# The rows of seven products moved by 180 bytes, and a fourth place in one ring of weights

## The chip, the cores and the metric

The kernel runs on one core of a Trainium2 chip. The metric is the device time of one execution in microseconds; the time given for a kernel is the median of its runs. TensorE (PE) multiplies matrices out of on-chip memory (SBUF) into accumulators (PSUM). VectorE (DVE), ScalarE (ACT) and GpSimd (POOL) work elementwise. SyncE (SP) issues most DMAs; POOL issues the accumulating ones. Each engine takes its own instructions in the order of its queue and waits at semaphores for the others.

## The reference, cut to what matters

One layer of a decoder: 512 tokens, model width 1024, feed-forward width 2816.

```python
def swiglu(x, w_in, w_out):
    a, b = jnp.split(x @ w_in, 2, axis=-1)
    return (jax.nn.silu(a) * b) @ w_out

h = x
h = h + 0.5 * swiglu(rmsnorm(h, ffn1_norm), ffn1_w_in, ffn1_w_out)
h = h + hybrid_mixer(rmsnorm(h, mix_norm), w_in, ...)   # HGRN2 and Gated DeltaNet branches
h = h + 0.5 * swiglu(rmsnorm(h, ffn2_norm), ffn2_w_in, ffn2_w_out)
y = rmsnorm(h, final_norm)
```

All is float32. The change touches the two feed-forward stages above all; the mixer shares their weight places.

## The kernel before, in words

**Three matmuls for one.** A float32 operand is split into a high part, rounded to the format that TensorE takes at full rate (float32r), and a remainder. `mm3` multiplies high by high, high by remainder and remainder by high into one accumulator. In its three lines (195, 196, 197) the stationary operand of the first two is a weight's high part, `whi`, and that of the third its remainder, `wlo`.

**Fast products.** A feed-forward stage computes the first `slow` of its 22 blocks of hidden columns plainly (5 in the first stage, of which two run in an opening of their own, 3 in the second). The others go through `fast`: the two-by-two block product of weights and activations is done as seven products of sums and differences (Strassen's scheme in Winograd's form) instead of eight. The seven activation operands are made once for a stage by `operands` and stand in the tile `xs` (28 rows of 512 columns; four rows for an operand, two of high parts and two of remainders). The matmuls of the fast part write `px` and move 256 columns each.

One product of `fast` is seven *units*, each of 4 x 3 matmuls on one 128 x 512 slab of weights:

| unit | weights | ring | how its remainder is made |
|---|---|---|---|
| 0 | a11 as loaded | 1 | fold |
| 1 | s2 = s1 - a11, s1 = a21 + a22 | 0 | VectorE |
| 2 | a12 as loaded | 1 | fold |
| 3 | s1 | 0 | VectorE |
| 4 | s3 = a11 - a21 | 0 | VectorE |
| 5 | s4 = a12 - s2 | 0 | VectorE |
| 6 | a22 as loaded | 1 | fold where product p < 7 or 15 <= p < 21, else VectorE |

The sums s1 to s4 are VectorE instructions of `comb` (line 371), into four tiles `sw`. For each unit ScalarE casts the slab to `whi` (line 334). Then either VectorE subtracts (`wlo`, line 313), or ScalarE writes the negated high part into `wlo` (line 338) and POOL issues a DMA that adds the weights from memory to it (line 339): the *fold*. The weights of `px` are kept in places of a ring; each ring has three places (WB // 2) for high parts and three for remainders. `pair` hands out the places, 576 columns wide, of which a unit uses 512 from column `off`: 0 for plain units and the mixer, SHIFT = 19 columns (76 bytes) for units of `fast`.

**What sets the order.** `stream` writes out all queues by hand. For each unit t it issues the unit's matmuls, then the functions in `posts[t]` (the product's own follow-up: the copy `p` after unit 0, `fa` after unit 2, its silu after 3, `uu` and `vb` after 4, `uc` after 6, its silu after the next unit 0, and two half-tile gate products, line 473, after the next unit 1; for products from 17 on also the split of the gate into `uh` and `ul`, lines 476 and 477). Then comes `ahead(t, 2)`, which prepares later units: remainders of the units cast in the call before, loads of raw weights (SP), sums for units up to t + COMB - 1 whose weights have been asked for, and then, ring 1 before ring 0, casts of units up to t + LEAD - 1 as far as their ring has a place: unit number m of a ring may be cast once unit m - 3 of the same ring has run.

**After the fast part** the stage multiplies the gated columns by its second weight matrix. The gated columns are split into high part and remainder by `split`, from the sixth-last unit of the fast part on, into rows of `xs` that are no longer read, in the order of the list `freed`.

Of the kernel before, what the change touches and what calls it, by code (L numbers as in the profile page):

```python
# [9 lines left out]
F32R = mybir.dt.float32r  # L10
# [6 lines left out]
P = 128  # L17
T = 512
# [21 lines left out]
WB = 6  # L40
# [14 lines left out]
LAG = dict(raw=3.5, gb=6.5, nb=6, m=7, out=5.5, back=6, turn=5.5)  # L55
EASE = 2.5
TURNED = (0, 1)
SHIFT = 19
LANES = {"a": 2, "b": 2, "d": 1, "e": 1}


# [85 lines left out]
def body(tc, xT, cst, sqc, hmask, dta, w1o, w1a, w2a, wt, wn, wab, wbh, wbg, wo, w1b, w2b, gfin, y, dbg=None):  # L147
# [4 lines left out]
    wp = ctx.enter_context(tc.tile_pool(name="wp", bufs=1))  # L152
# [22 lines left out]

    taken = [0]

    def pair(lane=None, off=0):

        taken[0] += 1  # L180
        n = "wv"[taken[0] % 2 if lane is None else lane]
        return [wp.tile([P, 576], F32R, tag=n + x, name="w" + x, bufs=WB // 2)[:, off:off + 512] for x in ("lo", "hi")]

    def slab(src):
        f = src.shape[-1]
# [73 lines left out]
    class Raw:  # L259

        def __init__(self, src, readers=1, fast=False):
            self.src, self.left, self.fast = src, readers, fast

    class Unit:

        def __init__(self, raws, operand, run, comb=None, drop=(), fold=None, lane=None, off=0):
            self.raws, self.operand, self.run, self.comb, self.drop, self.fold = raws, operand, run, comb, drop, fold
            self.lane, self.off = lane, off

    def plain(src, nk, xs, where, n=T, fold=False, roomy=lambda k: False):  # L270

# [12 lines left out]
            return Unit([raw], lambda: raw.tile[:, :w_ * P], run, drop=(raw,), fold=raw.src if fold and k >= fold - 1 else None)  # L284
        return [unit(k) for k in range(0, nk, 4)], held

    def stream(units, fp, early, hooks, posts):

        waiting = [r for u in units for r in u.raws]
        sent = {False: [], True: []}  # L290
        for i, u in enumerate(units):
            u.lane = i % 2 if u.lane is None else u.lane
        lanes = [[i for i, u in enumerate(units) if u.lane == l] for l in range(2)]
        done, combs, parts, fresh = [0, 0], [0], [None] * len(units), []
        room = [99]

        def loads():
            while waiting and room[0]:
                r = waiting[0]
                n = sent[r.fast]  # L300
                m = RW if r.fast else RB
                if len(n) >= m and n[-m].left:
                    break
                r.tile = fp.tile([P, T], F32, name="rw", bufs=RW) if r.fast else \
                    wp.tile([P, T], F32, tag="raw", name="raw", bufs=RB)
                sp.dma_start(r.tile[:, :r.src.shape[-1]], r.src)
                n.append(waiting.pop(0))
                room[0] -= 1

        def ahead(t, most):  # L310
            for i in fresh:
                x, hi, lo = parts[i]
                dve.tensor_tensor(lo, x, hi.bitcast(F32), op=ALU.subtract)  # L313
                for r in units[i].drop:
                    r.left -= 1
            fresh.clear()
            room[0] = 2
            loads()
            while combs[0] < min(t + COMB, len(units)) and not any(r in waiting for r in units[combs[0]].raws):
                if units[combs[0]].comb:  # L320
                    units[combs[0]].comb()
                    loads()
                combs[0] += 1
            for l in (1, 0):
                for _ in range(most):
                    m = done[l]
                    i = lanes[l][m] if m < len(lanes[l]) else len(units)
                    if i >= min(t + LEAD, len(units)) or i >= combs[0] and units[i].fold is None or \
                            any(r in waiting for r in units[i].raws) or m >= WB // 2 and lanes[l][m - WB // 2] > t:
                        break  # L330
                    x = units[i].operand()
                    f = x.shape[-1]
                    lo, hi = (y[:, :f] for y in pair(l, units[i].off))
                    act.copy(hi, x)  # L334
                    parts[i] = x, hi, lo
                    if units[i].fold is not None:

                        act.mul(lo, hi.bitcast(F32), -1.0)  # L338
                        pool.dma_start(lo, units[i].fold, accum_op=ALU.add)  # L339
                        for r in units[i].drop:  # L340
                            r.left -= 1
                    else:
                        fresh.append(i)
                    done[l] += 1
            loads()
        loads()
        for i in range(early):
            ahead(-1, 1)
        for t, u in enumerate(units):
            for f in hooks.get(t, ()):  # L350
                f()
            assert parts[t] and t not in fresh, t
            u.run(*parts[t][1:])
            for f in posts.get(t, ()):
                f()
            ahead(t, 2)
        assert not waiting

    def fast(w, p, xo, fp, at, posts, gate):
# [7 lines left out]
        def comb(n, x, y, op):  # L367
            def f():
                a, b = (z.tile if isinstance(z, Raw) else v[z] for z in (x, y))
                v[n] = fp.tile([P, T], F32, name="sw", bufs=SW)  # L370
                dve.tensor_tensor(v[n], a, b, op=op)  # L371
                for z in (x, y):
                    if isinstance(z, Raw):
                        z.left -= 1
            return f

        def prod(o, c, new=None):
            def run(hi, lo):
                if new:
                    v["pt"] = psc.tile([P, T], F32, tag="p" + new, name="px", bufs=LANES[new]) if new != "m" else \  # L380
                        psd.tile([P, T], F32, tag="mm", name="px")
                for i in range(4):
                    k = slice(i * P, (i + 1) * P)
                    mm3(v["pt"][:, one[c]], hi[:, k], lo[:, k], xo[o][0][:, i], xo[o][1][:, i], i == 0, i == 3)
            return run
# [31 lines left out]
        for t, f in ((0, f0), (2, f2), (3, f3), (4, f4), (6, f6), (7, f7), (8, f8)):  # L417
# [1 line left out]
        raw = lambda x: lambda: x.tile  # L419
        of = lambda n: lambda: v[n]  # L420
        s1, s2 = comb("s1", a21, a22, ALU.add), comb("s2", "s1", a11, ALU.subtract)
        us = [
            Unit([a11, a21], raw(a11), prod(0, 0, "m"), drop=(a11,), fold=a11.src, lane=1),
            Unit([a22, a12], of("s2"), prod(2, 0, "a"), lane=0, comb=lambda: (s1(), s2())),
            Unit([], raw(a12), prod(3, 1), drop=(a12,), fold=a12.src, lane=1),
# [1 line left out]
            Unit([], of("s3"), prod(4, 0), lane=0, comb=comb("s3", a11, a21, ALU.subtract)),  # L427
            Unit([], of("s4"), prod(5, 1, "m"), lane=0, comb=comb("s4", a12, "s2", ALU.subtract)),
            Unit([], raw(a22), prod(6, 0), drop=(a22,), fold=a22.src if 15 <= p < KF - 1 or p < 7 else None, lane=1)]
        for u in us:  # L430
            u.off = SHIFT
        return us

    def operands(c0, xs, rooms, start, hooks):

# [20 lines left out]
    def ffn(w1, w2, c0, after, slow, lead=None, last=None):  # L456

        with tc.tile_pool(name="ff", bufs=1) as fp, \
                tc.manual_schedule(engines={x.engine for x in (pe, act, dve, pool, sp)}):
            room = lambda n, m, dt=F32: fp.tile([P, m, T], dt, tag="room" + n, name="room" + n)  # L460
            rooms = dict(a=room("a", 8), b=room("b", 9))
            xs = fp.tile([P, 28, T], F32R, name="xs")
            units, posts, hooks = [], {}, {}
            on = lambda t, f: posts.setdefault(t, []).append(f)
            mm = lambda: psd.tile([P, T], F32, tag="mm", name="pmm")
            lane = lambda x: lambda: psc.tile([P, T], F32, tag="p" + x, name="pmm", bufs=LANES[x])
# [12 lines left out]
            def columns(pts, n, p, eng=dve, mul=dve):  # L479

                v = [None, None]

                def scale(i):
                    def f():
                        pt = pts[i]()
                        v[i] = fp.tile([P, T], F32, name=n[i], bufs=2 - i)
                        eng.tensor_tensor(v[i], pt, rbc, op=ALU.mult)
                    return f
                return (scale(0), scale(1), lambda: act.activation(v[0], v[0], AF.Silu),
                        lambda: gate(p, v[:1], v[1:], mul))  # L490
            done = 0
            if lead is not None:
# [3 lines left out]
                for p in range(2):  # L496
                    f = columns([lambda x=x: x for x in pts[2 * p:2 * p + 2]], ("fa", ("uu", "uc")[p]), p)
# [6 lines left out]
            for p in range(done, slow):  # L504
                us = []
                for n in range(2):
                    x, held = plain(w1[ORDER[p], n], KD, ux, lane("a" if lead is None else "b") if p == done and (lead is None or n == 0) else mm, fold=FOLD1[lead is None][p], roomy=lambda k: n if lead is not None or p else 0)
                    units += x
                    us.append((len(units) - 1, held))
                f = columns([lambda x=x: x["pt"] for _, x in us], ("fa", "uc"), p)  # L510
# [5 lines left out]
            for p in range(slow, KF):  # L516
                units += fast(w1, p, xo, fp, len(units), posts, gate)

            end = len(units)
            go, moved = [None] * KF, [None] * KF  # L520
            freed = [xs[:, k] for o in (0, 2, 3, 1, 4, 5, 6) for k in range(4 * o, 4 * o + 4)]

            def split(p):

# [11 lines left out]
                go[ORDER[p]] = moved[ORDER[p]] = uh[:, 24 - p], ul[:, 24 - p]  # L536
            if last is not None:
                last(w2, go, fp, rooms, units, on, part, freed)
                stream(units, fp, 3, hooks, posts)
                return  # L540
            for p in range(17):
                on(end - 6 + p if p < 6 else end + (p - 6) // 3, part(p))
# [9 lines left out]
            for d in range(KD):  # L552
                x, held = plain(w2[d], KF, lambda k, d=d: go[k] if d < 2 else moved[k], mm, fold=FOLD2 * (d == 0),
                                roomy=lambda k, d=d: d < 2 and k % 8 == 4)
# [5 lines left out]
                on(len(units) - 1, close)  # L560
                if d == 0:
                    on(len(units) - 1, move)
            stream(units, fp, 2, hooks, posts)

    def nextnorm(c0, spill=None, defer=False, **sqt):
        def after(d, pl):
# [1558 lines left out]
```

## Time and profile before

| | |
|---|---|
| median of 3 runs | 1567.69 us (1566.35 to 1568.27) |
| profiled execution | 1566.75 us, span 1564.9 us |
| mean granted TensorE clock | 0.999 |
| fast products | 17 from 61.8 us on, 19 from 1253.5 us on |
| largest groups of ScalarE and VectorE in the fast part | casts of sums, 144; remainders of sums, 144 |

A row of the profile's groups gives line, engine, operation, what is written and read (`out<-in`), shapes and count; then busy time and the mean of one, then the engine's idle time just before these instructions and what ended it. A wait for several semaphores is put down to the one that came last. A row of a timeline gives start and duration in microseconds. A row of a stretch gives its bounds and length, then busy time and count of PE, weight loads, DVE, ACT and POOL, the granted clock, the share of the DMA engines and GB/s (with a tile named, those of its instructions alone, without engines that have none).

### The profile page before, as it was taken

The numbers are of one execution on the slowest core, as the hardware profiler recorded it, in microseconds if no ns is written. First come the engines' busy times: TensorE is split into PE (matmuls) and PEld (weight loads), VectorE is DVE, ScalarE is ACT, GpSimd is POOL, SyncE is SP. The second block draws the span as 40 slices with busy tenths as digits, with TensorE's granted clock in tenths as the row PEclk, the third lists the DMA queues.
The fourth block names the chain that finished last, engine by engine and source line by source line (L and its number), as shares of the span: only waits on it lengthen the run. The fifth ranks groups of instructions, "written<-read, shape, count | busy, mean of one in ns | idle before, by whom it ended". The sixth has DMA issues, their size and how long they took to land.

```text
span 1564.9 us, 28718 instructions
## 1 busy us (share of the span) xinstructions
PE 1553.3 (99%) x10388; PEld 1339.6 (86%) x10388; DVE 1130.3 (72%) x2190; ACT 846.2 (54%) x1893; POOL 395.6 (25%) x713
## 2 busy tenths in 40 slices
PE   9999999999999999999999999999999999999998
PEld 8899998888888888888888888888888899999886
DVE  6988895438776778668888887865555799988323
ACT  5766764334354255557676676555324576676322
POOL 0211212100221222436534656440001221121000
PEclk9999999999999999999999999999999999999999
DMA  5777863333313123654463665556554598787431
GB/s 195 168 170 165 183 154 105 115 114 106 92 45 99 56 82 109 195 176 147 138 209 119 191 216 169 176 182 197 159 176 129 127 203 192 192 189 188 136 108 54
DMA packets 155645, 231.74 MB, mean 148 GB/s; under 512 B 22880, under 2 KB 53728, under 8 KB 155504
## 3 DMA queue, kind: packets, MB, share of 16 engines
q1 hardware_dynamic: 138512, 199.63, 40.7%
q0 software_dynamic: 14112, 25.70, 10.6%
q10 hardware_dynamic: 2880, 4.59, 1.0%
q8 instruction: 81, 1.33, 0.3%
q14 instruction: 60, 0.49, 0.1%
HBM read 200.73 MB, written 29.13 MB: 147 GB/s over the span
## 4 chain that ended last, share of the span: by engine, by line
PE 85%; DMA 6%; issue 5%; DVE 2%; ACT 1%; POOL 1%; SPq 0%; POOLq 0%; ACTq 0%; DVEq 0%
PE pmm L195 17%; PE pmm L196 16%; PE pmm L197 16%; PE pnat L195 4%; PE pnat L197 4%; PE px L197 4%; PE pnat L196 4%; PE px L195 4%; PE px L196 4%; DMA wlo<-w1b 3%; DMA wlo<-w1a 2%; PE pog L1531 1%; PE pgq L1323 1%; PE pw L1515 1%; PE pl L1070 1%
## 5 line engine op out<-in xcount | busy, mean ns | idle before, releaser
L195 PE MATMUL pmm<-uh,whi 128*128 128x512 f32 x830 | 342.4, 413 | 0.3 <-ACT tg L1629 0.2
L197 PE MATMUL pmm<-uh,wlo 128*128 128x512 f32 x830 | 324.7, 391 | 0.0
L196 PE MATMUL pmm<-ul,whi 128*128 128x512 f32 x830 | 324.1, 390 | 0.0
L197 PE MATMUL px<-xs,wlo 128*128 128x256 f32 x1008 | 279.9, 278 | 3.3 <-DMA wlo<-w1a 2.0
L195 PE MATMUL px<-xs,whi 128*128 128x256 f32 x1008 | 278.4, 276 | 0.0
L196 PE MATMUL px<-xs,whi 128*128 128x256 f32 x1008 | 278.3, 276 | 0.0
L1896 DVE TENSOR_TENSOR wlo<-raw,whi 128x512 fp32r<-128x512 f32 x226 | 158.9, 709 | 90.3 <-ACT whi L1894 87.2
L1894 ACT CAST whi<-raw 128x512 fp32r<-128x512 f32 x226 | 139.0, 619 | 129.7 <-PE pmm L196 95.7
L197 PEld LDWEIGHTS px<-xs,wlo 128*128 128x128 f32 x1008 | 189.2, 188 | 5.7 <-DMA wlo<-w1a 2.5
L195 PEld LDWEIGHTS px<-xs,whi 128*128 128x128 f32 x1008 | 189.2, 188 | 0.1
L196 PEld LDWEIGHTS px<-xs,whi 128*128 128x128 f32 x1008 | 189.2, 188 | 0.1
L197 PEld LDWEIGHTS pmm<-uh,wlo 128*128 128x128 f32 x830 | 155.7, 188 | 34.1
L195 PEld LDWEIGHTS pmm<-uh,whi 128*128 128x128 f32 x830 | 156.1, 188 | 31.4 <-ACT tg L1629 0.6
L196 PEld LDWEIGHTS pmm<-ul,whi 128*128 128x128 f32 x830 | 156.3, 188 | 28.7 <-DVE ul L1595 0.4
L334 ACT CAST whi<-sw 128x512 fp32r<-128x512 f32 x144 | 87.7, 615 | 82.5 <-DVE sw L371 66.2
L334 ACT CAST whi<-rw 128x512 fp32r<-128x512 f32 x153 | 94.3, 617 | 67.3 <-PE pnat L197 42.4
L313 DVE TENSOR_TENSOR wlo<-sw,whi 128x512 fp32r<-128x512 f32 x144 | 98.4, 683 | 0.0
L334 ACT CAST whi<-raw 128x512 fp32r<-128x512 f32 x71 | 42.5, 602 | 92.4 <-PE pmm L196 40.6
L313 DVE TENSOR_TENSOR wlo<-raw,whi 128x512 fp32r<-128x512 f32 x67 | 51.1, 778 | 48.5 <-ACT whi L334 48.5
L1374 POOL TENSOR_TENSOR fm<-gfs,gln 128x60 f32<-128x60 f32 (+24 forms) x155 | 60.7, 392 | 92.7 <-DMA od<-zo 26.6
L339 POOL DMA_DIRECT2D wlo<-w1b x52 | 45.0, 865 | 154.9 <-ACT wlo L338 126.8
L339 POOL DMA_DIRECT2D wlo<-w1a x46 | 39.9, 868 | 148.2 <-ACT wlo L338 128.9
(493 smaller groups left out, 3298.0 us busy)
## 6 DMA issues: line engine op xcount, KB each, us to landing
raw<-wt SPq DMA_DIRECT2D x160, 256.0 KB
rw<-w1b SPq DMA_DIRECT2D x80, 256.0 KB
rw<-w1a SPq DMA_DIRECT2D x74, 256.0 KB
wlo<-w1b POOLq DMA_DIRECT2D x52, 256.0 KB, 5.2
wlo<-w1a POOLq DMA_DIRECT2D x46, 256.0 KB, 5.2
raw<-w2a SPq DMA_DIRECT2D x36, 256.0 KB
raw<-wn SPq DMA_DIRECT2D x32, 256.0 KB
raw<-wbg SPq DMA_DIRECT2D x32, 256.0 KB
```

Source lines behind the costliest of these rows:

```text
L195: pe.matmul(pt, ah, bh, start=first, stop=False)
L196: pe.matmul(pt, ah, bl, start=False, stop=False)
L197: pe.matmul(pt, al, bh, start=False, stop=last)
L313: dve.tensor_tensor(lo, x, hi.bitcast(F32), op=ALU.subtract)
L334: act.copy(hi, x)
L339: pool.dma_start(lo, units[i].fold, accum_op=ALU.add)
L1070: pe.matmul(pl_[s0:s0 + 32, c * 16:(c + 1) * 16], ke[:, c * P + s0:c * P + s0 + 32], qv[:, c, r, :, 1], start=True, stop=True)
L1323: pe.matmul(pq[:, (c % 2) * 256:(c % 2) * 256 + 256], kq[:, c, 0], kq[:, c].rearrange("p a b -> p (a b)"), start=True, stop=True)
L1374: pool.tensor_tensor(tv, bc(m[:, j + 1:, j], w), t[:, j:j + 1, :w].to_broadcast([P, n, w]), op=ALU.mult)
L1515: pe.matmul(pw[:, hd2[i]], ut[:, 4 * i + c], xs[i], start=True, stop=True)
L1894: act.copy(hi, raw)
L1896: dve.tensor_tensor(lo, raw, hi.bitcast(F32), op=ALU.subtract)
```

## The change

1. SHIFT no longer moves the weights. `pair` gives 512 columns from the start of a place, and places are 512 columns wide instead of 576.
2. The rows of `xs` move instead: the tile `xt` is 64 columns longer, and `xs` is its part from column SHIFT = 45 (180 bytes) on. A second view, `xe`, begins at column 0; the rows that `freed` gives to `split` are those of `xe`. Row k of `xe` overlaps rows k - 1 and k of `xs`, and the order of `freed` is changed to fit.
3. Ring 0 (units 1, 3, 4 and 5 of a product, and every other plain unit) gets a fourth place, the two tiles `spare`. DEPTH = 4, 3 takes the place of WB // 2 in the test for a free place; every fourth unit of ring 0 uses `spare`.

```diff
-SHIFT = 19
+SHIFT = 45
+DEPTH = 4, 3
...
-    def pair(lane=None, off=0):
+    def pair(lane=None):
 
         taken[0] += 1
         n = "wv"[taken[0] % 2 if lane is None else lane]
-        return [wp.tile([P, 576], F32R, tag=n + x, name="w" + x, bufs=WB // 2)[:, off:off + 512] for x in ("lo", "hi")]
+        return [wp.tile([P, 512], F32R, tag=n + x, name="w" + x, bufs=WB // 2) for x in ("lo", "hi")]
...
-    def stream(units, fp, early, hooks, posts):
+    def stream(units, fp, spare, early, hooks, posts):
...
-                            any(r in waiting for r in units[i].raws) or m >= WB // 2 and lanes[l][m - WB // 2] > t:
+                            any(r in waiting for r in units[i].raws) or m >= DEPTH[l] and lanes[l][m - DEPTH[l]] > t:
                         break
                     x = units[i].operand()
                     f = x.shape[-1]
-                    lo, hi = (y[:, :f] for y in pair(l, units[i].off))
+                    lo, hi = (y[:, :f] for y in (spare if m % DEPTH[l] >= WB // 2 else pair(l)))
                     act.copy(hi, x)
...
-        for u in us:
-            u.off = SHIFT
-        return us
...
-            xs = fp.tile([P, 28, T], F32R, name="xs")
+            xt = fp.tile([P, 28 * T + 64], F32R, name="xs")
+            xs, xe = (xt[:, c:c + 28 * T].rearrange("p (a b) -> p a b", b=T) for c in (SHIFT, 0))
+            spare = [fp.tile([P, T], F32R, name="ws" + x) for x in ("lo", "hi")]
...
-            freed = [xs[:, k] for o in (0, 2, 3, 1, 4, 5, 6) for k in range(4 * o, 4 * o + 4)]
+            freed = [xe[:, k] for k in (*range(4), *range(9, 16), *range(4, 9), *range(16, 28))]
```

More of the change, by code (lines that the diff above doesn't have):

```diff
@@ L264, in body, with __init__ @@
     class Unit:
-        def __init__(self, raws, operand, run, comb=None, drop=(), fold=None, lane=None, off=0):
+        def __init__(self, raws, operand, run, comb=None, drop=(), fold=None, lane=None):
             self.raws, self.operand, self.run, self.comb, self.drop, self.fold = raws, operand, run, comb, drop, fold
-            self.lane, self.off = lane, off
+            self.lane = lane
     def plain(src, nk, xs, where, n=T, fold=False, roomy=lambda k: False):
@@ L421, in fast @@
         s1, s2 = comb("s1", a21, a22, ALU.add), comb("s2", "s1", a11, ALU.subtract)
-        us = [
+        return [
             Unit([a11, a21], raw(a11), prod(0, 0, "m"), drop=(a11,), fold=a11.src, lane=1),
@@ L538, in ffn @@
                 last(w2, go, fp, rooms, units, on, part, freed)
-                stream(units, fp, 3, hooks, posts)
+                stream(units, fp, spare, 3, hooks, posts)
                 return
@@ L562, in ffn @@
                     on(len(units) - 1, move)
-            stream(units, fp, 2, hooks, posts)
+            stream(units, fp, spare, 2, hooks, posts)
     def nextnorm(c0, spill=None, defer=False, **sqt):
```

## The prediction

> **What bounds the kernel now.** I read the page's engine shares and costliest groups first, then stretches of the span, then the groups that touch the tile px, and last the timeline of one product, queue by queue.
>
> ```profile
> span 1564.9 us, 28718 instructions
> PE 1553.3 (99%) x10388; PEld 1339.6 (86%) x10388; DVE 1130.3 (72%) x2190; ACT 846.2 (54%) x1893; POOL 395.6 (25%) x713
> L197 PE MATMUL px<-xs,wlo 128*128 128x256 f32 x1008 | 279.9, 278 | 3.3 <-DMA wlo<-w1a 2.0
> ```
> ```profile
> 80.88:157.04 76.16, 76.16 (x674) 76.16 (x673) 67.92 (x121) 50.36 (x97) 13.81 (x16) 1.00 0.72 167
> ```
> ```profile
> 61.80:227.60 165.80, 163.63 (x1428) 162.50 (x1427) 41.55 (x67) 6.07 (x17) 1.00 0.79 176
> 1253.50:1437.90 184.40, 183.15 (x1596) 181.74 (x1596) 46.37 (x75) 6.76 (x19) 1.00 0.85 196
> ```
> ```profile
> L195 PE MATMUL px<-xs,whi x1008: 276/276/285, 61.8 to 1437.5; 128*128 128x256 f32 x168
>   DMA wlo<-w1a: 4.5, 6
>   DVE wlo L313: 2.7, 8
>   DMA wlo<-w1b: 1.3, 3
> ```
>
> TensorE is the bound: 99% busy. The second fence (stretch, its length, then busy time and count of PE, weight loads, DVE, ACT, POOL) is eight fast products without a gap: 76.16 us for 8 x 84 matmuls, so 113.3 ns each, 1.36 us for a unit of twelve, 9.52 us for a product of seven units. The third fence takes px alone over both fast stages: 1428 matmuls would need 161.8 us and have 165.8, 1596 would need 180.9 and have 184.4. The fast parts thus lose about 7.4 us to waits, and no more is to be won there. The last fence says on what (its weight loads counted too): 5.8 of 8.5 on fold DMAs, 2.7 on VectorE's remainders, those of the ring that the change deepens; in proportion 5.0 and 2.4 of the 7.4 us.
>
> In those eight products neither VectorE (67.92 of 76.16 us) nor ScalarE (50.36) is full, but they hand work to each other. One product on ScalarE, VectorE, POOL and the first matmul of its unit 1:
>
> ```profile
> 120.63 0.42 ACT L412 ACTIVATE uc<-uc 128x256 f32<-128x256 f32 x1 [0.61 <-DVE uc L390]
> 120.95 0.36 ACT L395 COPY p<-px 128x256 f32<-128x256 f32 x1
> 121.21 0.63 ACT L334 CAST whi<-rw 128x512 fp32r<-128x512 f32 x1
> 121.87 0.63 ACT L338 ACTIVATE wlo<-whi 128x512 fp32r<-128x512 f32 x1
> 122.40 0.60 ACT L334 CAST whi<-sw 128x512 fp32r<-128x512 f32 x1
> 123.13 0.62 ACT L334 CAST whi<-rw 128x512 fp32r<-128x512 f32 x1
> 123.79 0.63 ACT L338 ACTIVATE wlo<-whi 128x512 fp32r<-128x512 f32 x1
> 124.44 0.42 ACT L401 ACTIVATE fa<-fa 128x256 f32<-128x256 f32 x1
> 124.76 0.60 ACT L334 CAST whi<-sw 128x512 fp32r<-128x512 f32 x1
> 128.40 0.62 ACT L334 CAST whi<-sw 128x512 fp32r<-128x512 f32 x1 [1.93 <-DVE sw L371]
> 128.93 0.62 ACT L334 CAST whi<-rw 128x512 fp32r<-128x512 f32 x1
> ```
> ```profile
> 121.72 0.42 DVE L473 TENSOR_TENSOR rooma<-fa,uc 128x256 f32<-128x256 f32 x1
> 122.05 0.42 DVE L473 TENSOR_TENSOR rooma<-uc,vb 128x256 f32<-128x256 f32 x1
> 122.39 0.69 DVE L371 TENSOR_TENSOR sw<-rw 128x512 f32<-128x512 f32 x1
> 123.11 0.69 DVE L371 TENSOR_TENSOR sw<-sw,rw 128x512 f32<-128x512 f32 x1
> 127.63 0.69 DVE L371 TENSOR_TENSOR sw<-rw 128x512 f32<-128x512 f32 x1
> 128.23 0.69 DVE L313 TENSOR_TENSOR wlo<-sw,whi 128x512 fp32r<-128x512 f32 x1
> 128.83 0.68 DVE L371 TENSOR_TENSOR sw<-rw,sw 128x512 f32<-128x512 f32 x1
> ```
> ```profile
> 122.79 0.86 POOL L339 DMA_DIRECT2D wlo<-w1a  x1 [6.74 <-ACT wlo L338]
> ```
> ```profile
> 120.32 0.28 PE L195 MATMUL px<-xs,whi 128*128 128x256 f32 x1
> ```
> ```profile
> ACT whi L334 <- DVE sw L371: 17.4, 9, 1.9
> ```
>
> ScalarE stands still once in each product, 1.9 us, at the cast of unit 4, until VectorE has made its sum s3 (127.63 + 0.69; cast at 128.40; the last row counts these waits over the eight products). All behind it in ScalarE's queue waits too, and POOL issues a fold only after its negation. The casts of units 1, 3 and 5 find their sums ready.
>
> **The change, part by part.** *The fourth place.* After each unit t, `ahead` forms sums for units up to t + 7 (COMB = 8) and casts units up to t + 8 whose sum is formed and whose place is free. With three places in ring 0 a cast comes after the unit three ring places earlier: unit 1 is cast 5 units ahead of its use, 3 and 4 six, 5 four. With four, all are cast 7 ahead, for units 1, 4 and 5 in the very call that issues their sums. Kinds and number of instructions stay; so do fold casts, DMAs and loads in SP's and POOL's order. What moves is ScalarE's order: after unit 1 runs it gets the next unit 1, whose two sums VectorE was handed a moment ago, in place of a unit 5 summed long before; after unit 4 the cast of unit 4, after unit 5 that of unit 5. So three casts wait for sums, not one, each with fold casts behind it.
>
> That closes a loop through both queues. Its steps, end to end, from the rows above: a cast after its sum 0.71 (0.09 + 0.62); a remainder after its cast 0.71 (0.68, and 0.03 that I estimate for the handover); a VectorE instruction right behind another 0.60 (128.23 to 128.83); a cast behind other ScalarE work 0.52; a negation 0.67 (121.84 to 122.50); a silu 0.32; each half of the gate 0.33; s2 after s1 0.72 (122.39 to 123.11).
>
> From one s3 to the next, where unit 6 isn't folded: cast 4 0.71, remainder 4 0.71, s4 0.60, cast 5 0.71, cast 6 0.52, remainder 6 0.71, gate 0.66, s1 0.60, s2 0.72, cast 1 0.71, cast 2 0.52, negation 2 0.67, silu 0.32, cast 3 0.52, remainder 3 0.71, s3 0.60: 9.99 us against TensorE's 9.52, so 0.47 late in each product. Today's loop, in which casts 5 and 1 wait for nothing, is cast 4, cast 6, silu, copy (0.26), cast 0, negation, cast 5, cast 2, negation, silu, cast 1, remainder 1, s3: 6.9 us, and TensorE sets the pace.
>
> Where unit 6 is folded (products 3 to 6 and 15 to 20), negation, silu and half a gate (0.67 + 0.32 + 0.45) stand for remainder and half a gate (0.71 + 0.33): 10.39, or 0.87 late. Where the gate of a product from 17 on is split, two more instructions lie in the loop:
>
> ```profile
> L476 ACT CAST uh<-g x10: 603/605/622, 190.5 to 1443.5; 128x512 fp32r<-128x512 f32 x10
> ```
> ```profile
> L477 DVE TENSOR_TENSOR ul<-g,uh x10: 691/692/693, 191.2 to 1444.2; 128x512 fp32r<-128x512 f32 x10
> ```
>
> That cast stands behind copy, cast 0 and negation 0 and ahead of s1. From cast 6: 0.67 + 0.32 + 0.26 + 0.52 + 0.67 + 0.51 + 0.72 + 0.60 + 0.72 = 4.99 to the end of s2 instead of 3.09: 12.29, 2.77 late, and 2.10 where unit 6 isn't folded (product 21).
>
> How much lateness TensorE forgives: a fold of unit 0 is cast at 121.21, 0.89 after its place came free at 120.32, and issued at 122.79, 2.47 after; it is needed at the third matmul of the unit seven later, 6 x 1.36 + 0.23 = 8.39 after.
>
> ```profile
> DMA to landing us min/median/max: 4.0/4.6/5.5
> ```
> ```profile
> DMA to landing us min/median/max: 4.1/6.1/7.7
> ```
>
> Landing takes 4.6 us in the median from 80 to 150 us, so 1.3 us is spare; from 158 to 216 us, where unit 6 is folded too, 6.1, and nothing is (today's stalls).
>
> Sum. First stage: products 7 to 14, 8 x 0.47 = 3.8; 6 and 15 to 18, 5 x 0.87 = 4.4; 19 and 20, 5.5; 21, 2.1; together 15.8, less 1.3 forgiven once: 14.5. Second stage, with 4 and 5 also folded: 3.8 + 7 x 0.87 + 7.6 - 1.3 = 16.2. The 5.0 us lost to late DMAs stay, the 2.4 of remainders go: 30.7 - 2.4 = +28.3 us. Ends for the loop: with handovers of nothing (seven in a loop, about 0.05 each) 0.35 less for 34 products, -12; with the landings of the folded products at their maximum, 7.7 for 6.1, in half of some 16, +12.
>
> *The shift.* Rows stood at 0 and weights at 76 bytes; now 180 and 0. The difference changes by 256 bytes. Places of a ring are 2304 bytes apart, nine times 256, and px has 276 ns as minimum and as median over all of them, so multiples of 256 show no effect: 0. Ends: nothing below (no px is shorter), 9 ns (285) for each of 3024, 27 us, above; in the loop's shadow (9.52 + 0.76 = 10.28 against 10 to 12.3) about 5 of it would show. I take 0, the row with nearly all the px. The Trainium skill, SBUF — State Buffer, Specifications (TRN2), speaks against the change: lines are 16 bytes, and each step to a new line costs. Rows at 180 would start 4 bytes into a line and touch 65 lines for 64; an estimate from that page is 1/64 of 113.3 ns, 5.4 us over all px, where the sum above has 0. No run here shows rows so placed; weights at 76 bytes are as crooked, and their loads hide under the matmuls.
>
> *Widths, `xe` and `freed`.* Rings of 512 columns for 576 and two spare tiles change addresses only: 0, by the same px row. The new `freed` order lets splits write rows that units 2 and 3 of the last product read last, three units earlier: no wait, 0. Plain units are cast up to 2 units earlier into freer queues: 0.
>
> The profiled execution took 1566.75 us (span 1564.9), 0.94 under the median of 1567.69. With +28.3 it gives 1595.0, and the median 1596.0.
>
> **The rivals.** *(A) The deeper ring pays.* If the lateness stays under what TensorE forgives, cast 5 comes 7 units ahead, the remainder waits go and a share of the DMA waits: 1567.69 - 2.4 to - 7.4, 1560.3 to 1565.3. It decides if the loop is under 9.52 us, that is, if 0.5 us of my 9.99 overlaps. For it: 2.7 us of px waits are VectorE remainders, and VectorE has 8.2 us free in eight products. Against: the 1.9 us wait in each product shows that a cast issued close to its sum stops the queue.
>
> *(B) Crooked rows are slower.* Without the loop and with every px at the longest of its row, 285 for 276 ns, 1567.69 + 27.2 - 2.4 = 1592.5; it makes the kernel measurably slower from (3.1 + 2.4) / 3024 = 1.8 ns for each matmul on. Nothing in px speaks for it, since its rows have always stood at 0. By the page's estimate above it would be 1570.7. With the loop it mostly hides.
>
> *(C) The loop and the DMAs add up*: landings near 7.7 us with folds bunched by late casts, 1596 + 12 = 1608. For it the 6.1 median; against it, products that take 10 to 12 us leave the DMA queues more room.
>
> *(D) The place isn't used earlier*, since sums come 7 units ahead at most: 1567.7. Against it: 7 is more than today's 4 to 6.
>
> **How the numbers follow.** Forecast (loop) 0.72, C 0.10, A 0.10, B 0.05, D 0.03. 0.2% (3.1 us) is about what this kernel's timing can tell from no change. A splits evenly between faster and same; D is same; B is slower but for 0.01. Faster 0.05, same 0.09, slower 0.86. The forecast's own range is 1584 to 1608; reaching towards B below and past C above: 1578 to 1612.
>
> **What would show it.** Right: ScalarE's casts of sums wait for VectorE's sums three times in each product, not once; fast products take about 10 us from 7 to 14 and near 12 at 19 to 21; px waits are for fold DMAs, none for remainders; px stays at 276 ns; 113.3 ns holds between waits; the slow products and the mixer keep their times. Wrong: products at 9.52 (A), or px over 276 (B).

## The result, and the profile after

The changed kernel takes **1611.15 us** (median; 1608.91 to 1615.18) against 1567.43 for the kernel before on the same chips: a ratio of 1.0283, 95% interval 1.0273 to 1.0294, or 43.7 us more. The forecast was 1596.0 with a range of 1578 to 1612: slower, and within the range, but 15 us over its centre and only 0.85 us under its upper end. The execution that was profiled took 1615.18 us, the longest of the six; its mean granted TensorE clock was 0.995, that of the shortest 0.999.

Lines of the page of the kernel after: the span, the engines' shares, the shares of the chain that ended last, and two groups.

```profile
span 1613.4 us, 28753 instructions
PE 1585.0 (98%) x10388; PEld 1367.9 (85%) x10388; DVE 1137.8 (71%) x2190; ACT 838.6 (52%) x1893; POOL 396.1 (25%) x713
...
PE 80%; DVE 6%; issue 5%; DMA 4%; ACT 4%; POOL 1%; SPq 0%; ACTq 0%; POOLq 0%; DVEq 0%
...
L198 PE MATMUL px<-xs,wlo 128*128 128x256 f32 x864 | 250.0, 289 | 15.7 <-DMA wlo<-w1b 10.9
...
L335 ACT CAST whi<-sw 128x512 fp32r<-128x512 f32 x108 | 67.0, 621 | 157.3 <-DVE sw L372 144.5
```

The same two views of the kernel before:

```profile
PE 85%; DMA 6%; issue 5%; DVE 2%; ACT 1%; POOL 1%; SPq 0%; POOLq 0%; ACTq 0%; DVEq 0%
...
L334 ACT CAST whi<-sw 128x512 fp32r<-128x512 f32 x144 | 87.7, 615 | 82.5 <-DVE sw L371 66.2
```

TensorE has the same 10388 matmuls and stays the bound, but VectorE and ScalarE now hold 10% of the chain that ended last (3% before). The casts of sums are the heart of it: ScalarE stands still 144.5 us ahead of 108 of them, for VectorE's sums, where it stood still 66.2 us ahead of 144. (The other 36 write the spare place and stand in a row of their own.)

The same two views of px as in the prediction, stretches first (the whole fast part of the first stage, its products 7 to 14, and the whole fast part of the second stage), then the groups of the tile:

```profile
62.30:241.40 179.10, 174.25 (x1428) 172.25 (x1428) 40.36 (x65) 6.00 (x17) 1.00 0.74 162
83.25:163.98 80.73, 80.73 (x674) 80.72 (x673) 19.86 (x32) 2.82 (x8) 1.00 0.69 157
1274.60:1486.60 212.00, 200.97 (x1596) 196.86 (x1596) 45.04 (x73) 6.70 (x19) 0.98 0.74 170
```
```profile
L196 PE MATMUL px<-xs,whi x864: 278/282/415, 62.3 to 1486.0; 128*128 128x256 f32 x173
...
  DMA wlo<-w1b: 25.3, 31
  DMA wlo<-w1a: 11.3, 15
```

The fast parts take 179.1 and 212.0 us where they took 165.8 and 184.4. Two things are to be seen. The stretch of products 7 to 14 is full (80.73 of 80.73), and yet takes 80.73 us for what took 76.16: each px matmul is longer, 282 ns for 276. Outside that stretch TensorE waits, and only for fold DMAs; no remainder of VectorE's is left among the waits.

Below, **excess** is a product's time from its first px matmul to the next product's first, less the 9.52 us of 84 matmuls at 113.3 ns; sums over 17 products in the first stage and 19 in the second are given as a pair, worked out from the starts of the px matmuls in each trace. Before: 3.9 + 3.4. After: 17.1 + 30.8, so 40.6 us of the 48.5 that the span grew; 7.9 lie outside the fast parts.

### The profile page after: what moved, and what is told of

It reads as the page before. It is cut to its first block, busy times and chain, and to the rows that moved or that the text cites. A ratio compares the mean times of both kernels' runs of the same rounds, so it can differ in the third digit from the quotient of the medians.

```text
span 1613.4 us, 28753 instructions
## 1 busy us (share of the span) xinstructions
PE 1585.0 (98%) x10388; PEld 1367.9 (85%) x10388; DVE 1137.8 (71%) x2190; ACT 838.6 (52%) x1893; POOL 396.1 (25%) x713
## 4 chain that ended last, share of the span: by engine, by line
PE 80%; DVE 6%; issue 5%; DMA 4%; ACT 4%; POOL 1%; SPq 0%; ACTq 0%; POOLq 0%; DVEq 0%
PE pmm L196 17%; PE pmm L197 16%; PE pmm L198 16%; PE pnat L196 4%; PE pnat L198 4%; PE pnat L197 4%; PE px L198 3%; PE px L196 3%; PE px L197 3%; DMA wlo<-w1b 2%; DVE sw L372 2%; ACT whi L335 2%; DVE wlo L314 1%; DMA rw<-w1b 1%; DMA wlo<-w1a 1%
## 5 line engine op out<-in xcount | busy, mean ns | idle before, releaser
L198 PE MATMUL px<-xs,wlo 128*128 128x256 f32 x864 | 250.0, 289 | 15.7 <-DMA wlo<-w1b 10.9
L196 PE MATMUL px<-xs,whi 128*128 128x256 f32 x864 | 245.9, 285 | 0.0
L197 PE MATMUL px<-xs,whi 128*128 128x256 f32 x864 | 245.5, 284 | 0.0
L1896 DVE TENSOR_TENSOR wlo<-raw,whi 128x512 fp32r<-128x512 f32 x226 | 158.8, 709 | 86.4 <-ACT whi L1894 82.9
L1894 ACT CAST whi<-raw 128x512 fp32r<-128x512 f32 x226 | 139.0, 619 | 131.0 <-PE pmm L197 92.0
L198 PEld LDWEIGHTS px<-xs,wlo 128*128 128x128 f32 x864 | 164.5, 190 | 21.4 <-DMA wlo<-w1b 14.4
L196 PEld LDWEIGHTS px<-xs,whi 128*128 128x128 f32 x864 | 166.2, 192 | 0.1
L197 PEld LDWEIGHTS px<-xs,whi 128*128 128x128 f32 x864 | 165.3, 191 | 0.1
L335 ACT CAST whi<-sw 128x512 fp32r<-128x512 f32 x108 | 67.0, 621 | 157.3 <-DVE sw L372 144.5
L335 ACT CAST whi<-rw 128x512 fp32r<-128x512 f32 (+1 forms) x145 | 88.9, 616 | 57.3 <-PE pnat L198 40.3
L314 DVE TENSOR_TENSOR wlo<-sw,whi 128x512 fp32r<-128x512 f32 x108 | 74.7, 692 | 35.7 <-ACT whi L335 26.5
L1374 POOL TENSOR_TENSOR fm<-gfs,gln 128x60 f32<-128x60 f32 (+24 forms) x155 | 65.4, 422 | 91.5 <-DMA gln<-hmask 40.6
L335 ACT CAST whi<-raw 128x512 fp32r<-128x512 f32 (+1 forms) x65 | 38.2, 603 | 86.3 <-PE pmm L197 41.2
L314 DVE TENSOR_TENSOR wlo<-raw,whi 128x512 fp32r<-128x512 f32 (+1 forms) x61 | 46.6, 783 | 41.0 <-ACT whi L335 41.0
```

The lines of the kernel that those rows point to most:

```text
L196: pe.matmul(pt, ah, bh, start=first, stop=False)
L197: pe.matmul(pt, ah, bl, start=False, stop=False)
L198: pe.matmul(pt, al, bh, start=False, stop=last)
L1374: pool.tensor_tensor(tv, bc(m[:, j + 1:, j], w), t[:, j:j + 1, :w].to_broadcast([P, n, w]), op=ALU.mult)
L1894: act.copy(hi, raw)
L1896: dve.tensor_tensor(lo, raw, hi.bitcast(F32), op=ALU.subtract)
```

## The experiments

All times are medians beside runs of the kernel before on the same chip (1566.1 to 1567.0 us).

| kernel | us | ratio to before, 95% | excess, us |
|---|---|---|---|
| rows by 180 bytes, three places | 1581.57 | 1.0081 to 1.0111 | 10.5 + 12.3 |
| fourth place alone | 1608.32 | 1.0252 to 1.0282 | 15.2 + 28.1 |
| rows and weights at 0 | 1581.43 | 1.0081 to 1.0111 | 10.1 + 11.4 |
| rows 192, weights 0 | 1573.40 | 1.0027 to 1.0061 | 7.1 + 8.3 |
| fourth place, sums a unit earlier | 1581.76 | 1.0081 to 1.0111 | 6.3 + 8.2 |
| fourth place, no plain fold in stage 2 | 1606.97 | 1.0246 to 1.0283 | 16.5 + 28.8 |
| fourth place, no transposes | 1604.40 | 1.0228 to 1.0258 | 15.8 + 19.8 |
| rows 4, weights 80 | 1583.82 | 1.0097 to 1.0130 | 11.2 + 13.1 |
| rows 176, weights 0 | 1579.68 | 1.0066 to 1.0094 | 9.6 + 11.1 |
| fourth place, sums 2 earlier, no plain fold | 1573.50 | 1.0026 to 1.0052 | 2.4 + 5.2 |
| before, sums a unit earlier | 1567.96 | 0.9994 to 1.0012 | 2.9 + 3.7 |
| rows 180, weights 76 | 1586.89 | 1.0111 to 1.0148 | 13.0 + 14.7 |

### The two halves of the change

Rows alone (the changed kernel with three places):

```diff
-DEPTH = 4, 3
+DEPTH = 3, 3
```

> The changed kernel with three places in ring 0 again: rows at 180 bytes, weights at 0, order of the queues as before. Theory 1 (two costs: px 6.7 ns slower by the moved rows, and the loop of casts and sums): units of 1.44 us, three casts no longer waiting, 3024 x 6.7 ns = 20 us less some of the 7 us of waits that longer products hide: 1581 to 1588. Theory 2 (the moved rows are all of it): about 1605 to 1611. Theory 3 (the loop is all of it, and px is stretched only by what the waits leave behind): px at 276 ns and 1567.

The fourth place alone (the kernel before, weights at 76 bytes; room for the places comes from single buffers of `p1` and `vb`):

```diff
+DEPTH = 4, 3
...
-m >= WB // 2 and lanes[l][m - WB // 2] > t:
+m >= DEPTH[l] and lanes[l][m - DEPTH[l]] > t:
...
-lo, hi = (y[:, :f] for y in pair(l, units[i].off))
+lo, hi = (y[:, :f] for y in (spare if m % DEPTH[l] >= WB // 2 else pair(l, units[i].off)))
```

> The kernel before (weights at 76 bytes, rows at 0) with a fourth place in ring 0; room for it comes from single buffers for p1 and vb and a shorter tile edge. Theory 1: px at 276 ns, and the loop alone: products of about 10.0 us from 7 to 14 and 12 at 19 to 21, +28 us: 1585 to 1605. Theory 2: 1565 to 1568. Theory 3: the whole loss, 1605 to 1612.

A stretch of px for each: products 7 to 14 of the first stage with the rows alone, then both fast parts with the place alone.

```profile
82.53:163.16 80.63, 80.63 (x674) 80.63 (x673) 19.91 (x32) 2.85 (x8) 1.00 0.67 158
```
```profile
61.75:238.95 177.20, 167.67 (x1428) 163.95 (x1427) 40.30 (x65) 6.01 (x17) 1.00 0.70 162
1271.90:1481.10 209.20, 192.22 (x1596) 186.66 (x1595) 45.57 (x74) 6.71 (x19) 0.98 0.74 173
```

Both halves cost: 15.5 us for the rows, about 42 for the place, and 43.7 together. They overlap. With the rows alone TensorE is gapless and each px takes 120.0 ns from start to start (80.63 / 672); with the place alone px keeps 276 ns in the median and TensorE has holes. In the changed kernel a product of 10.08 us leaves the loop of about 10 us hidden behind it, so of the rows' 15.5 us only 1.5 show in the medians (43.7 against 42.2), 5 between the two profiled spans.

### What in the placing costs

Each of these has three places and moves only where rows and weights begin. In order: both at 0; rows 192 bytes, a multiple of 64; rows 4 and weights 80, which keeps the distance of before; rows 176, a multiple of 16; and the rows' half of the shift without the weights' half (its diff is against rows 4 with weights 80, that of 192 and of 176 against the rows alone).

```diff
-SHIFT = 19
+SHIFT = 0
```

> The kernel before with weights and rows both at 0. If what counts is the difference between the two places, px is slower here than at 76 bytes by 5 to 10 ns, 1582 to 1600. If only where rows stand counts (they are at 0), px stays at 276 ns and the time at 1567.

```diff
-SHIFT = 45
+SHIFT = 48
```

> As rows_only, with the rows at 48 columns (192 bytes, a multiple of 16 and 64) instead of 45. If the rows' own crookedness costs (4 bytes past a 16-byte step), px is back at 276 ns and the time at 1567. If the difference to the weights counts, px may be anywhere from 276 to 290 ns, and the time from 1567 to 1600.

```diff
-SHIFT = 19
+SHIFT = 20
+ROWS = 1
...
+xs, xe = (xt[:, c:c + 28 * T].rearrange("p (a b) -> p a b", b=T) for c in (ROWS, 0))
```

> The kernel before with rows at 4 bytes and weights at 80 instead of 0 and 76: the same difference, but the rows now start 4 bytes past a step of 16, as at 180. If crooked rows cost by themselves, px goes from 113 to 118 to 120 ns between starts: 1576 to 1585. If only the difference counts, 1567.

```diff
-SHIFT = 45
+SHIFT = 44
```

> Rows at 176 bytes (44 columns, a whole number of 16-byte steps) instead of 180, weights at 0, three places in each ring. If the 4 bytes past a 16-byte step are the whole cost of the shift, px comes back to 113.3 ns from start to start, and the time to before's, 1567 us (within 2). If the rows' distance from the weights counts as well, as with rows and weights both at 0 (120.0 ns, 1581.4 us) and rows at 192 bytes (117.8 or 113.3 ns, 1573.4 us), px lies between 115 and 120 ns in part of the products and the time at 1570 to 1581. If only the distance counts, and 4 bytes of it make no odds, it is as with 180 bytes: 120 ns, 1581.6.

```diff
-SHIFT = 20
-ROWS = 1
+SHIFT = 19
+ROWS = 45
```

> Rows at 180 bytes as after, weights at 76 bytes as before, three places: the half of the shift that moves the rows, without the half that moves the weights. In every kernel with slower px so far (weights at 0 with rows at 180, 0, 176 and 192 bytes; weights at 80 with rows at 4) the weights began on a 16-byte step, and in every one with 113.3 ns they began 12 bytes past one, with rows at 0. If it is the weights' start that counts, px is back at 113.3 ns and the time at 1566 to 1568. If rows 4 bytes past a step cost by themselves (as rows at 4 bytes seemed to show), px is at 118 to 121 ns and the time at 1577 to 1585.

The px group that reads high weights at line 196 of both 0/0 and rows 192, of rows 4 with weights 80, of rows 176, and of rows 180 with weights 76, in that order (duration minimum, median, maximum):

```profile
L196 PE MATMUL px<-xs,whi x1008: 278/283/288, 62.3 to 1451.8; 128*128 128x256 f32 x168
```
```profile
L196 PE MATMUL px<-xs,whi x1008: 276/281/286, 61.7 to 1445.0; 128*128 128x256 f32 x168
```
```profile
L196 PE MATMUL px<-xs,whi x1008: 281/287/288, 62.0 to 1453.8; 128*128 128x256 f32 x168
```
```profile
L196 PE MATMUL px<-xs,whi x1008: 279/281/287, 61.8 to 1450.5; 128*128 128x256 f32 x168
```
```profile
L196 PE MATMUL px<-xs,whi x1008: 282/285/289, 62.6 to 1457.8; 128*128 128x256 f32 x168
```

The product times give the rate more finely, from start to start of a px matmul (the value that each kernel has in most of its products):

| rows, bytes | weights, bytes | ns, start to start |
|---|---|---|
| 0 | 76 | 113.3 |
| 0 | 0 | 120.0 |
| 176 | 0 | 119.3 |
| 192 | 0 | 117.8, in some stretches 113.3 |
| 180 | 0 | 120.0, in some stretches 123.3 |
| 4 | 80 | 120.8 and 121.1 |
| 180 | 76 | 122.2, in one stretch 120.0 |

Of these seven placings, with three places, only that of the kernel before keeps 113.3 ns throughout. The first two rows differ in the weights alone, the first and the last in the rows alone: each step away costs by itself, 6.7 ns and 8.9 ns. Rows that begin off a 16-byte step were slow in all three kernels that had them, whatever the weights. Rows on such a step were slow too when the weights began on one. So the hope that 176 or 192 bytes would give the rate back fell (176 gives nearly none of it), and so did the theory that only the weights' start counts, on which the last run was set. Whether the weights' start or its distance from the rows makes 76 bytes good with rows at 0 stays open: no run moves the weights alone to another start off a 16-byte step. The distance by itself is not enough: rows 4 with weights 80 keep it. And the kernels with rows at 176, 180 and 192 and weights at 0 also have places of 512 columns for 576, which no run changes by itself.

The placing doesn't settle the rate alone. Behind a wait it can take another value and keep it up to the next wait, even with rows at 0 and weights at 76: without the plain fold (a kernel of the next section) products 4 to 6 of the second stage run at 120.0 ns. Product 5 of them, without a gap:

```profile
1292.31:1302.39 10.08, 10.08 (x86) 10.08 (x85) 2.44 (x4) 0.35 (x1) 1.00 0.85 204
```

What a wait changes there isn't shown.

### What in the fourth place costs

**The loop of sums and casts.** One unit more between a sum and its cast, with the fourth place alone:

```diff
-RW, SW, COMB, LEAD = 6, 4, 8, 9
+RW, SW, COMB, LEAD = 6, 4, 9, 9
```

> places_only with COMB = 9: sums are formed one unit earlier, so that a cast no longer stands right behind its own sum; casts and places stay. Theory 1 (the loop of casts and sums makes the waits): the loop falls under 9.52 us, products 7 to 14 return to 9.52 us, waits of ScalarE for sums shrink by more than half, and of the 36 us that the fast parts lost against the kernel before at least 25 come back: 1572 to 1583; 7 us outside the fast parts stay. Rival (a fourth place as such, by addresses or by crowding the DMA queues, costs the time): unchanged, 1603 to 1612.

Stretches of px with the fourth place and COMB = 9, both stages:

```profile
62.00:230.30 168.30, 163.90 (x1428) 162.46 (x1427) 40.74 (x66) 6.17 (x17) 1.00 0.76 171
1263.40:1452.70 189.30, 183.98 (x1596) 181.86 (x1596) 45.99 (x75) 6.79 (x19) 1.00 0.80 189
```

Nothing but the order changed, and the fast parts give back 28.8 of the 36.0 us that the place had cost them (43.3 to 14.5 of excess). Seven of the eight products 7 to 14 of the first stage are at 9.52 us again. That is the loop, shown. One thing expected didn't come: ScalarE's waits for sums were to shrink by more than half, and went from 27.5 to 21.9 us between 80.88 and 163.98 us, and from 137.1 to 85.5 in all. So the sum of these waits doesn't measure the cost; the product times fit a loop that costs only where it is longer than a product.

**Transposes in the second stage.** There the excess was 28.1 us, 13 more than in the first. In it VectorE has work that the first stage has not, eight transposes of the residual, in the middle of the fast part:

```profile
L663 DVE STREAM_TRANSPOSE rooma<-h x8: 1101/1108/1120, 1290.3 to 1365.8; 128x512 f32<-128x512 f32 x8
```

Without them (the rest as with the fourth place alone; this kernel leaves the residual unsorted, so its result isn't the layer's):

```diff
-                x = rooms["a"][:, d]
-                dve.transpose(x.rearrange("p (f t j) -> p f t j", f=4, t=NT),
-                              h[:, d].rearrange("p (t i f) -> p f t i", t=NT, f=4))
-                sp.dma_start(hn[d], x)
+                sp.dma_start(hn[d], h[:, d])
```

> places_only without the eight VectorE transposes of 1.1 us that the second stage makes in its products 4 to 11 (their rows go out as they stand, so the residual of the last block is left unsorted). Theory: each stands in the loop, ahead of uu and vb, and makes it 0.6 us longer; without them the second stage's products 4 to 11 lose 4 to 6 us less: 1602 to 1605. Rival (loads or fold landings make the second stage worse than the first): 1606 to 1610.

The second stage without them:

```profile
1273.15:1474.10 200.95, 187.90 (x1596) 183.22 (x1596) 45.29 (x73) 6.71 (x19) 1.00 0.78 179
```

209.2 became 201.0 us, and 8.3 of excess went. Not all of it is the transposes' own. The granted clock in the fast part is 1.00 here and was 0.98 with them, by two stretches at half clock:

```profile
1413.77:1417.18 3.41, 3.41 (x19) 3.41 (x18) 1.99 (x4) 2.72 (x6) 1.73 (x2) 0.50 0.80 212
1468.37:1471.78 3.41, 3.18 (x15) 3.18 (x16) 2.42 (x5) 1.21 (x3) 0.86 (x1) 0.50 0.55 77
```

In them px matmuls follow each other at 0.21 us for 0.113, about 1.5 us more in each stretch. That leaves some 5 us for eight transposes, about 0.65 us each: near the 0.6 expected, and not the full 1.1 us that one takes. The medians say the same: 3.9 us less, or 4.6 against before on the same chip. Only 2.8 of the 8.3 us went in products 4 to 11 themselves, where 4 to 6 were expected; the rest went in later ones.

**A fold ahead of the norm.** Outside the fast parts the profiled span also grew. At the head of the second stage POOL works on the norm's `rcol`, for which TensorE waits. POOL's timeline after:

```profile
1231.84 1.29 POOL L234 TENSOR_TENSOR acc<-acc,sqt 128x512 f32<-128x512 f32 x1 [4.15 <-ACT sqt L232]
1242.81 0.93 POOL L340 DMA_DIRECT2D wlo<-w1b  x1 [9.68 <-ACT wlo L339]
1243.47 1.33 POOL L258 TENSOR_TENSOR rcol<-msq,mhalf 128x4 f32<-128x4 f32 x1
```

A fold's DMA stands ahead of `rcol`; POOL is idle for 9.68 us before it, until ScalarE's negation. With four places a plain unit of the second stage is cast eight units ahead instead of six, and that fold came to stand here. Without folds in these plain units (and with the fourth place alone):

```diff
-FOLD1 = (0, 0, 0, 0, 1), (0, 0, 1)
+FOLD1 = (0, 0, 0, 0, 1), (0, 0, 0)
```

> places_only without folds in the slow products of the second stage (VectorE makes those four remainders). Theory: at the head of the second stage a fold that is now cast two units earlier stands in POOL's queue ahead of the power that the norm needs; TensorE waits 2.5 us for it and its clock falls to about half for some 3.5 us. Without the fold both go: 4 us faster than places_only, 1602 to 1606. Rival (the wait is ScalarE's or VectorE's): no change, 1607 to 1610.

```profile
1229.91 1.29 POOL L234 TENSOR_TENSOR acc<-acc,sqt 128x512 f32<-128x512 f32 x1 [4.15 <-DMA hr<-hd]
1237.95 1.43 POOL L258 TENSOR_TENSOR rcol<-msq,mhalf 128x4 f32<-128x4 f32 x1 [6.75 <-DMA raw<-w1b]
```

From the last `acc` to `rcol` are 8.04 us, as before, instead of 10.88 with the fourth place alone (11.63 after), and from that `acc` to the first px 38.7 us instead of 42.6 (38.5 before). So the 4 us expected are there, and the place is shown. The whole gained only 1.35 us in the median, within its scatter, at the edge of what the rival allowed: the fast parts of the profiled execution lost 2.0 more, with four stretches at half clock for two, and with the products at 120.0 ns shown above.

**Both repairs together**, with sums two units earlier:

```diff
-RW, SW, COMB, LEAD = 6, 4, 8, 9
-FOLD1 = (0, 0, 0, 0, 1), (0, 0, 1)
+RW, SW, COMB, LEAD = 6, 4, 10, 9
+FOLD1 = (0, 0, 0, 0, 1), (0, 0, 0)
```

> Before with the fourth place alone (weights stay at 76 bytes), but sums formed up to two units earlier (COMB = 10 for 8), and without the fold of the plain unit of the second stage. If the fourth place costs only through the loop of sums and casts and through POOL's fold at the head of the second stage, both are gone: fast parts within 8 us of TensorE's own time, the gap of 2.8 us at the head of the second stage gone, the whole within 1566 to 1572. If more of the cost lies elsewhere (9 units gave 1581.8), it stays at 1576 to 1582.

```profile
61.80:226.30 164.50, 163.41 (x1428) 162.38 (x1428) 41.25 (x67) 6.17 (x17) 1.00 0.76 173
1255.80:1442.05 186.25, 184.08 (x1596) 182.48 (x1596) 46.25 (x75) 6.73 (x19) 1.00 0.81 191
```

The fast parts together are where they were before (7.6 us of excess for 7.3), so the loop and the fold account for some 36 of the place's 42 us (and the single buffers of `p1` and `vb`, which are still there, cost the fast parts nothing). 6.5 us remain in the median, a little over what was expected. In the profiled execution 3.7 lie between the two fast parts. Of the five executions the two with a granted clock of 0.999 and 1.000 took 1570.6 and 1571.1 us, the three with 0.998 took 1573.5 to 1575.0. Even so mended, the fourth place gains nothing.

**The wait that seemed worth removing.** Sums a unit earlier in the kernel before:

```diff
-RW, SW, COMB, LEAD = 6, 4, 8, 9
+RW, SW, COMB, LEAD = 6, 4, 9, 9
```

> Before, with sums formed one unit earlier (COMB = 9 for 8), three places, weights at 76 bytes. ScalarE's 1.9 us wait in each product, at the cast of unit 4, is for a sum handed over a moment ago; one unit earlier it should go. If that wait holds up the fold casts that TensorE waits for (part of the 7.4 us that the fast parts lose), 1560 to 1565 us; if TensorE's waits are the landings' own time, no change, 1567; if earlier sums take VectorE from other work, 1568 to 1572.

ScalarE's waits in products 7 to 14, complete; there were 17.4 us for VectorE's sums:

```profile
ACT whi L334 <- PE px L196: 20.3, 32, 0.7
ACT uc L412 <- DVE uc L390: 2.9, 8, 0.4
ACT fa L401 <- DVE fa L390: 0.5, 2, 0.2
```

The 1.9 us wait of each product is gone, and the time is the same (0.9994 to 1.0012). ScalarE now waits for a place instead. Nothing that TensorE needed was held up by that wait; no version beat the kernel before.

## Why the prediction was right, and where it was off

**The range: met at its edge.** 1611.15 lies under the upper end of 1612, which was drawn past rival C, and C's mechanism didn't happen. That the time fell inside the range is in part luck: the loop came as worked out, and beside it stand costs that the prediction put at 0.

**The loop: right, at its size.** The prediction said three waits of ScalarE in each product, not one. The waits from 80.88 to 163.98 us (products 7 to 14 begin at 83.25) and ScalarE's timeline of one product, after:

```profile
ACT whi L335 <- DVE sw L372: 31.7, 23, 2.2
```
```profile
119.48 0.62 ACT L335 CAST whi<-sw 128x512 fp32r<-128x512 f32 x1 [1.13 <-DVE sw L372]
...
121.50 0.60 ACT L335 CAST wshi<-sw 128x512 fp32r<-128x512 f32 x1
123.52 0.62 ACT L335 CAST whi<-sw 128x512 fp32r<-128x512 f32 x1 [1.42 <-DVE sw L372]
125.56 0.62 ACT L335 CAST whi<-sw 128x512 fp32r<-128x512 f32 x1 [1.42 <-DVE sw L372]
...
129.59 0.62 ACT L335 CAST whi<-sw 128x512 fp32r<-128x512 f32 x1 [1.13 <-DVE sw L372]
```

Casts of units 1, 4 and 5 wait, that of unit 3 does not, as worked out: 23 waits in eight products. Its price can be read where px keeps its rate, in the fourth place alone, first stage: products 7 to 14 lost 3.4 us (3.8 predicted), 6 and 15 to 18 lost 4.8 (4.4), 19 and 20 lost 5.9 (5.5), 21 lost 1.0 (2.1). Together 15.1 against 15.8.

**The sum around the loop: two small errors of opposite sign.** The prediction took off 1.3 us a stage as forgiven and kept 5.0 us of DMA stalls on top, over both stages. In the first stage neither shows: the 15.2 us are about the loop's terms alone. That the remainder waits go (2.4 us) was right.

**The second stage: mis-sized.** Predicted were 16.2 us, and 28.1 came with the place alone. One term left out is VectorE's transposes: of the loop's instructions the prediction listed those of a product of `fast`, and not what `posts` puts between them in this stage. They cost some 5 us. Another is the clock: "113.3 ns holds between waits" failed, as two stretches at half clock cost some 3. Of the other 4 us, 1.3 are those taken off as forgiven; the rest wasn't traced.

**"Plain units are cast up to 2 units earlier into freer queues: 0", and the fold DMAs' order on POOL that was to stay: failed.** POOL's queue was not free: a DMA that had stood behind `rcol` came ahead of it. From the last `acc` to the first px of the second stage it was 4.3 us longer in the profile of after (42.8 for 38.5). The prediction's rows of POOL were all from the fast parts.

**"The slow products and the mixer keep their times": failed at one more place.** With a fourth place, the first plain matmuls behind the fast part wait for the split of the gated columns. TensorE's timeline there, after:

```profile
251.88 0.51 PE L196 MATMUL pmm<-xs,wshi 128*128 128x512 f32 x1 [1.64 <-ACT xs L530]
...
253.71 0.63 PE L196 MATMUL pmm<-xs,wshi 128*128 128x512 f32 x1
254.14 0.63 PE L197 MATMUL pmm<-xs,wshi 128*128 128x512 f32 x1
...
256.37 0.39 PE L197 MATMUL pmm<-xs,whi 128*128 128x512 f32 x1
256.60 0.40 PE L198 MATMUL pmm<-xs,wlo 128*128 128x512 f32 x1
```

The wait is 1.64 us, and the slower matmuls behind it add to it: the first output block closes 3.0 us later after the last px (19.3 us, before 16.3). The loop's late casts are not the cause: the wait stays where the loop is gone. With COMB = 9 and the fourth place:

```profile
PE pmm L196 <- ACT xs L533: 2.0, 1, 2.0
```

With sums two units earlier it is still 1.48 us, and the block closes 1.7 us later than before. With the rows alone there is no such wait. So it comes with the fourth place; which cast or split then stands in the way wasn't traced.

**The shift: the term that was wrong in kind.** The prediction took 0, since multiples of 256 bytes show no effect and the change moves the difference by 256. The rows of the kernel before never left one placing, so its trace could say nothing on another: rows 180 with weights 0 differ from rows 0 with weights 76 by those 256 bytes, and a px matmul takes 6.7 ns more. Alone the shift costs 15.5 us, inside the bounds of 0 and 27, and 1.5 (medians) to 5 (profiles) of it show beside the loop, where the prediction's bound had "about 5". The Trainium skill, SBUF — State Buffer, Specifications (TRN2), says that each crossing to a new 16-byte line costs, and the prediction drew an estimate of 5.4 us from it; the sign agrees, the size does not (15.5), and rows at 0 or 176 bytes, which cross no extra line, were as slow with the weights at 0.

**The rivals.** A and D are out: the casts come earlier and wait. B, crooked rows, is true beside the forecast, not instead of it. C had nearly the time (1608) for another reason. Landings became shorter, not longer (medians of 4.1 and 5.0 us in the two stretches of the prediction, for 4.6 and 6.1). What adds to the loop is the transposes, POOL's order, the wait at the split, the half clock behind such waits, and the rows.

## What to carry to other kernels

Before giving a producer more room, follow the chain that fills it: a cast that may come earlier waits for a sum that doesn't, and in a queue kept in order everything behind it waits too; if you deepen the ring, form its inputs as many steps earlier (COMB = 9 gave back 27 us). When two engines close a loop near the bound's pace, list every instruction in it, those of other work too: a transpose of 1.1 us that stood in it cost some 0.65 us. Moving where operands begin in memory is a change of its own: it took a matmul from 113.3 to 120.0 ns here, and a trace in which they never moved can't price it. And a wait on an engine that isn't the bound is no promise: taking away 1.9 us in each product gained nothing.

## What the runs showed of the hardware

**Where rows and weights begin changes TensorE's rate, together.** From 113.3 to 122.2 ns for the same matmul of 256 columns in float32r. Moving only the weights from 76 bytes to 0 took it to 120.0, though weight loads run beside the matmuls. The Trainium skill, TensorE: Matmul & The Clock Gate, Step-by-step: what each phase is for, has weights and moving rows on two read ports, so that loading weights takes no bandwidth from a running matmul; here the rate depends on the weights' start all the same. Whether the loads hold up the matmuls or set the pace themselves isn't shown: in the eight products of before they are as gapless as the matmuls (76.16 us of 76.16), and one takes 188 ns there and 192 with rows and weights at 0 (medians).

**The rate has more than one value for one placing, and changed only at a wait.** It was 117.8 or 113.3 ns with rows at 192 bytes, 120.0 or 123.3 with rows at 180 and weights at 0, and with the placing of before 113.3, but 120.0 in products 4 to 6 of the second stage without the plain fold.

**A wait of 1.6 us can halve the clock for 3.4 us.** Two stretches after, behind the waits for the split and for `rcol`, and the second of these waits:

```profile
252.56:255.97 3.41, 3.28 (x8) 2.60 (x9) 3.41 (x7) 3.41 (x8) 0.00 (x0) 0.50 0.13 21
1245.84:1249.25 3.41, 3.41 (x10) 2.69 (x9) 2.01 (x3) 0.58 (x1) 0.00 (x0) 0.50 0.41 111
```
```profile
PE pbc L249 <- POOL rcol L258: 2.4, 1, 2.4
```

The granted clock is 0.50 over 3.41 us, and matmuls of 512 columns follow each other at 0.43 us (253.71 to 254.14) instead of 0.23 (256.37 to 256.60); some eight of them 0.2 us longer add about 1.6 us to a wait. Two more such stretches lie in the second fast part. The length of the wait doesn't decide it alone. With COMB = 9 and the fourth place TensorE waited longer at both points, 1.97 us and 2.60 us, and kept its clock; the stretches right behind:

```profile
241.14:245.14 4.00, 3.63 (x13) 2.47 (x14) 4.00 (x8) 4.00 (x8) 0.00 (x0) 1.00 0.09 13
1235.09:1239.09 4.00, 4.00 (x22) 3.45 (x23) 2.01 (x3) 0.86 (x2) 0.00 (x0) 1.00 0.50 119
```

The Trainium skill, TensorE: Matmul & The Clock Gate, Why this matters for your kernels, warns of gaps over about 3 us; here waits of 1.64 us at the split and 2.4 us at `rcol` were followed by half clock, so shorter ones can be enough.
